# Index gather and gate weights of an expert layer in 16 bits, on VectorE alone

## The chip, the cores and the metric

The kernel runs on one core of a Trainium2 chip. Its metric is the time of one execution on the device in microseconds (us), the median of several runs. The engines are TensorE (PE; its weight loads are a row of their own, PEld), VectorE (DVE), ScalarE (ACT), GpSimd (POOL) and SyncE (SP), which here issues the loads. Each works through its own list of instructions in a fixed order; semaphores hold an instruction until its inputs are there and its output buffer is free.

## The reference, cut to what matters

The reference is two transformer blocks on 256 tokens of width 1024 in float32. The change lies in the last part of the second block, a feed-forward layer of product-key experts:

```python
q = (xb @ w_query).reshape(t, 8, 2, 64)              # 8 heads, 2 key halves
s = einsum('thpd,hpkd->thpk', q, sub_keys)           # 128 keys for each half
top_s, top_i = top_k(s, 16)
cand_s = top_s[:, :, 0, :, None] + top_s[:, :, 1, None, :]        # 16 x 16
cand_i = top_i[:, :, 0, :, None] * 128 + top_i[:, :, 1, None, :]
best_s, best_pos = top_k(cand_s, 16)
idx = take_along_axis(cand_i, best_pos, -1)          # 16 of 16384 experts
gate = softmax(best_s)
act = gelu(einsum('td,thkd->thk', xb, expert_down[idx]))
y = einsum('thk,thkd->td', gate * act, expert_up[idx])
```

## The kernel before, in words

The kernel doesn't fetch single experts. It multiplies all tokens with all 16384 rows of both expert tables and puts the gates in between as a matrix W, which is zero for every expert that a token did not choose. An expert's number is 128 i + j, with i from the first key half and j from the second. W lies with j on the 128 partitions, then i, then the token: 128 x 128 x 256, in two halves of 64 i (`W0`, `W1`).

**Weight stream.** All weights come in granules of 128 x 1024 float32 (`granule`, lines 199 to 216). SP loads one into `raw`; ACT rounds it to the format of the products (`wh`, line 214); a subtraction gives the rest (`wl`, line 215). A product is then the sum of three matmuls: wh with the high part of the other operand, wh with its low part, wl with the high part. `wl` runs on DVE, except where `B.share` is 2: then every second granule's goes to POOL. `raw` has 4 buffers, `wh` and `wl` 3 each.

**Down** (`down`, line 1204) takes two granules a step, 24 matmuls of 256 tokens for each (lines 239 to 241), and ACT writes the gelu of the sum into W. **Up** (`up`, line 1235) takes one granule for each i: ACT and DVE split W's row into `wsh` and `wsl` (lines 225 and 226), and 12 matmuls of 512 columns add to four accumulators that stay open over all 128 granules (lines 1248 to 1250).

**Selection** (`select`) runs beside the first half of down. For each of two blocks of 128 tokens it makes the scores (line 1120), sorts out the best 16 of each key half with `top16` (DVE, one input each), adds the 16 x 16 candidates on POOL (`cand`, line 1132) and sorts again. The index gather follows (lines 1140 to 1155): the position in the candidates gives two numbers of 0 to 15 (`pf`); each is compared with a `ramp` of 0 to 15, the result multiplied by the indices (`idf`) and summed over the 16 (`m`, 1024 elements of float32 at a time, four times a block). The end of a block transposes numbers and gates to (head, choice) on partitions (`finish`), and the gate times 4096 is split into two float16 parts.

**Gates** (`gates`, line 1212) go over 8 tokens at a time, 32 groups for each half of W. DVE compares i with a ramp (`eq`, 8 x 64) and j with a ramp (`a`, 8 x 128), both float16; ACT multiplies eq by the gate's high part, one instruction a token; POOL by its low part; PE adds, for each token, `a` (as weights) times `bh` (64 columns) for both parts (line 1227); DVE multiplies the PSUM result into W (line 1229), walking W by token, then i, so that neighbours are 1024 bytes apart.

The order of work comes from generators that are driven side by side with weights: `down(0)` with `select` (1.0 to 2.1), `down(64)` with `gates(0)` (1.0 to 1.25), `up(0)` with `gates(64)` (1.0 to 1.25), then `up(64)` alone. A scheduler with a cost model of its own then fixes the list of each engine.

Of the kernel before, what the change touches and what calls it, by code (L numbers as in the profile page):

```python
# [17 lines left out]
OP = mybir.AluOpType  # L18
# [13 lines left out]
# ---------------------------------------------------------------- host layout  # L32


def _blocks_b(w):
    """[K, N] -> granules [*, 128, 1024]: for each 128 columns all of K, on partitions."""
    k, n = w.shape
    g = w.reshape(k // P, P, n // P, P).transpose(2, 1, 0, 3)
    per = D // k
    g = g.reshape(n // P // per, per, P, k).transpose(0, 2, 1, 3)  # L40
    return g.reshape(-1, P, D)


def _blocks_a(w, width):
    """[K, N] -> granules [*, 128, 1024]: for each `width` columns, D / width chunks of K at a time."""
# [33 lines left out]
def pack(inputs):  # L79
# [38 lines left out]
    # by query (row, column): head, key row, key column  # L118
# [16 lines left out]
# ---------------------------------------------------------------- helpers  # L135


def bc(ap, n):
    """A view with an inner dimension of stride 0."""
    return bass.AP(tensor=ap.tensor, offset=ap.offset, ap=[list(s) for s in ap.ap] + [[0, n]])  # L140


def bc_at(ap, pos, n):
    """A view with a dimension of stride 0 put before dimension `pos`."""
# [4 lines left out]
def drive(*gens):  # L149
    """Interleaves generators in proportion to the weights they come with."""  # L150
# [10 lines left out]
class Block:  # L161
# [15 lines left out]
    # ------------------------------------------------------------ constants  # L177
# [20 lines left out]
    # ------------------------------------------------------------ weight stream  # L198
    def granule(self, src, kept=None):
        """Loads [128, 1024] of weights; returns the two exact parts for float32r products."""  # L200
# [32 lines left out]
    def mm_cols(self, out, w, x, nk, first=True, last=True, off=0):  # L233
        """out[n, t] += W[k, n] X[k, t]; w: two [128, 1024] parts, columns off ... of them."""
# [8 lines left out]
    def mm_rows(self, outs, w, x, k0, nk, width, first, last, off=0, tiles=(0, 1)):  # L243
        """outs[i][t, n] += X[k, t] W[k, n] over nk chunks of K from k0 on."""
# [11 lines left out]
    # ------------------------------------------------------------ norms  # L256
    def rsqrt(self, v, pool, tag):
        """v^-0.5 of a few columns, by Newton steps from the exponent's half."""
# [18 lines left out]
    def gain(self, pool, name, tag, bufs=1):  # L277
        """A gain in every partition, times the root of the row length."""
# [11 lines left out]
    def total(self, pool, ss, tag):  # L290
        """sum of squares + D eps of both row blocks, from the sums over halves."""
# [4 lines left out]
    def scaled_cols(self, pool, src, r, g, x, width=512):  # L296
        """(src * r) * g, rows to columns, in two parts; r: a column of each row block."""
# [8 lines left out]
    def warm(self, n):  # L306
        """Keeps the tensor engine's clock up while it waits for a norm."""
# [7 lines left out]
    def turn(self, y, x, k0, n, i):  # L315
        """n blocks of 128 columns of y to the columns x, from block k0 on."""
# [7 lines left out]
# ---------------------------------------------------------------- first block  # L324


def first_block(B, rp):
    tc, nc, A = B.tc, B.nc, B.A
    with ExitStack() as es:
# [11 lines left out]
        # the gain in every partition, times the root of the row length  # L341
# [113 lines left out]
        def conv():  # L455
# [3 lines left out]
            # layer norm over the channels  # L459
# [81 lines left out]
        # relative position bias of every query and key; -1e30 outside the window  # L541
# [5 lines left out]
        # twice the merged branches  # L547
# [24 lines left out]
    # ---------------- feed-forward  # L572
    with ExitStack() as es:
# [40 lines left out]
        # the final norm of this block and the first of the next one:  # L614
        # x3 = x2 r2 gf with r2 = (v / D)^-0.5, v = sum x2^2 + D eps, and
        # h3 = x3 r3 g3 with r2 r3 = (u / D)^-0.5, u = sum (x2 gf)^2 + eps v
# [36 lines left out]
def rows_out(B, rp, name, X, res, scale, g, X2, pool, tags):  # L653
    """res + scale * (X^T W), as rows; its normed columns go to X2."""
# [32 lines left out]
# ---------------------------------------------------------------- second block  # L687


def rope_tables(B, cp, pool):  # L690
    """sin and cos of position * frequency, [128 t, 2, 8] each."""
# [11 lines left out]
    # ang - 2 pi n, with n the nearest integer and 2 pi in three parts  # L703
# [603 lines left out]
```

## Time and profile before

| | |
|---|---|
| time, median of 3 runs | 1481.1 us (1480.63 to 1483.35) |
| span of the profiled execution | 1484.5 us |
| mean granted TensorE clock | 0.991 |
| PE, PEld busy | 97%, 88% |
| DVE, ACT, POOL busy | 76%, 59%, 19% |
| selection beside `down(0)` | about 690 to 885 us |
| `gates(0)` beside `down(64)` | to about 1108 us |
| `gates(64)` beside `up(0)` | to about 1272 us |
| `up(64)`, end | to 1484.5 us |

The profile is one execution; the span is from its first to its last instruction, and no time beside the span was taken of that execution. Groups of instructions read: line, engine, operation, output<-inputs, shapes, count | busy us, mean ns of one | idle time of the engine just before them, and who ended it. The timeline reads: start, duration, engine, line, operation, count, and in brackets the idle time before it.

### The profile page before, as it was taken

The page shows a single profiled execution, that of the slowest core. Times are in us where ns is not written, and L with a number is a line of the kernel's source. Part 1 is how long each engine was busy: PE and PEld are TensorE (multiplying, and loading weights), DVE is VectorE, ACT ScalarE, POOL GpSimd, SP SyncE. Part 2 cuts the span into 40 slices and gives each one's busy share as a digit, 9 for nine tenths or more (in the row PEclk, how much of TensorE's full clock was granted, in tenths as well). Part 3 has the DMA queues.
Part 4 walks back from the last instruction along what each step waited for, and adds up shares of the span by engine and source line. Part 5 has one row for each costly group of instructions (what it writes and reads, how often), then busy time and mean ns, then how long its engine had stood idle before and what let it go on. Part 6 is the DMA issues. An engine that isn't in the chain of part 4 may idle for free.

```text
span 1484.5 us, 27008 instructions
## 1 busy us (share of the span) xinstructions
PE 1440.6 (97%) x10351; PEld 1302.6 (88%) x10351; DVE 1134.0 (76%) x1812; ACT 881.8 (59%) x1697; POOL 286.5 (19%) x253
## 2 busy tenths in 40 slices
PE   8899999999999999999989989999999999999998
PEld 7788989999898888989989989999997777888887
DVE  6987867768796667764877876999959999765665
ACT  6476566566554666444444446877757777555453
POOL 4543000000203000002434542222103433000000
PEclk9999999999999999999999999999999999999999
DMA  7534556556466333565544445455565545666664
GB/s 257 172 109 143 180 177 189 183 186 225 123 191 203 120 110 111 178 205 162 166 150 156 156 150 171 157 168 167 165 213 157 157 157 157 199 193 191 198 192 135
DMA packets 70117, 251.49 MB, mean 169 GB/s; under 512 B 8026, under 2 KB 8418, under 8 KB 69731
## 3 DMA queue, kind: packets, MB, share of 16 engines
q1 hardware_dynamic: 69698, 249.17, 52.9%
q8 instruction: 81, 1.33, 0.4%
q10 hardware_dynamic: 288, 0.59, 0.2%
q14 instruction: 50, 0.40, 0.1%
HBM read 247.63 MB, written 2.11 MB: 168 GB/s over the span
## 4 chain that ended last, share of the span: by engine, by line
PE 84%; DVE 12%; issue 2%; ACT 1%; DMA 0%; POOL 0%; SPq 0%; POOLq 0%; ACTq 0%; DVEq 0%
PE mm L239 15%; PE mm L241 15%; PE mm L240 15%; PE mm L1250 7%; PE mm L1248 7%; PE mm L1249 7%; DVE wl L215 3%; PE mm L253 2%; PE mm L254 2%; PE mm L252 2%; PE at L1227 2%; DVE y L441 2%; PE at L585 1%; PE at L586 1%; PE at L587 1%
## 5 line engine op out<-in xcount | busy, mean ns | idle before, releaser
L214 ACT ACTIVATE wh<-raw 128x1024 fp32r<-128x1024 f32 (+1 forms) x457 | 479.8, 1052 | 360.2 <-PE mm L240 273.3
L215 DVE TENSOR_TENSOR wl<-raw,wh 128x1024 fp32r<-128x1024 f32 x422 | 531.3, 1261 | 204.2 <-ACT wh L214 198.5
L241 PE MATMUL mm<-xh,wl 128*128 128x256 f32 x1952 | 559.3, 287 | 16.5 <-DVE wl L215 16.5
L239 PE MATMUL mm<-xh,wh 128*128 128x256 f32 x1952 | 562.2, 288 | 0.9 <-ACT xh L225 0.9
L240 PE MATMUL mm<-xl,wh 128*128 128x256 f32 x1952 | 558.9, 286 | 0.0
L241 PEld LDWEIGHTS mm<-xh,wl 128*128 128x128 f32 x1952 | 378.7, 194 | 20.9 <-DVE wl L215 18.9
L239 PEld LDWEIGHTS mm<-xh,wh 128*128 128x128 f32 x1952 | 379.0, 194 | 7.3 <-issue 2.9
L240 PEld LDWEIGHTS mm<-xl,wh 128*128 128x128 f32 x1952 | 379.0, 194 | 4.3 <-issue 3.3
L1250 PE MATMUL mm<-wh,wsl 128*128 128x512 f32 x512 | 200.8, 392 | 6.3 <-DVE wsl L226 6.3
L1248 PE MATMUL mm<-wh,wsh 128*128 128x512 f32 x512 | 201.8, 394 | 0.0
L1249 PE MATMUL mm<-wl,wsh 128*128 128x512 f32 x512 | 199.8, 390 | 0.1
L1221 POOL TENSOR_TENSOR bh<-eq,parts 128x512 f16<-128x512 f16 x64 | 100.4, 1578 | 274.3 <-PE at L1227 172.8
L1220 ACT ACTIVATE bh<-eq,high 128x64 f16<-128x64 f16 x512 | 128.7, 334 | 16.0 <-DVE eq L1217 15.3
L225 ACT ACTIVATE wsh<-W 128x256 fp32r<-128x256 f32 x128 | 53.2, 417 | 127.9 <-PE mm L1249 125.7
L1250 PEld LDWEIGHTS mm<-wh,wsl 128*128 128x128 f32 x512 | 96.1, 188 | 30.6 <-DVE wsl L226 10.4
L1249 PEld LDWEIGHTS mm<-wl,wsh 128*128 128x128 f32 x512 | 96.2, 188 | 20.6 <-DVE wl L215 1.1
L1248 PEld LDWEIGHTS mm<-wh,wsh 128*128 128x128 f32 x512 | 96.2, 188 | 18.6
L215 POOL TENSOR_TENSOR wl<-raw,wh 128x1024 fp32r<-128x1024 f32 (+1 forms) x35 | 86.8, 2481 | 121.3 <-ACT wh L214 120.7
L1229 DVE SCALAR_TENSOR_TENSOR W<-at,W 128x512 f32<-128x512 f32 x64 | 84.5, 1341 | 10.2 <-PE at L1227 10.2
L226 DVE TENSOR_TENSOR wsl<-W,wsh 128x256 fp32r<-128x256 f32 x128 | 53.5, 418 | 42.1 <-ACT wsh L225 42.1
L1223 DVE TENSOR_TENSOR a<-ramp,numbers 128x1024 f16<-128x1024 f16 x64 | 79.9, 1250 | 0.0
L446 POOL TENSOR_TENSOR y<-y,tap 128x256 f32<-128x256 f32 x60 | 58.5, 975 | 51.4 <-ACT tap L445 47.3
(343 smaller groups left out, 1740.1 us busy)
## 6 DMA issues: line engine op xcount, KB each, us to landing
raw<-in_ws_dram SPq DMA_DIRECT2D x199, 512.0 KB, 3.6
raw<-in_pd_dram SPq DMA_DIRECT2D x128, 512.0 KB, 3.6
raw<-in_pu_dram SPq DMA_DIRECT2D x128, 512.0 KB, 3.6
bias<-in_rpb_dram SPq DMA_DIRECT2D x2, 1024.0 KB, 7.7
x<-in_x_dram SPq DMA_DIRECT2D x4, 256.0 KB, 4.0
r_m<-in_rows_dram SPq DMA_DIRECT2D x2, 512.0 KB, 3.6
mb<-negm_d SPq DMA_DIRECT2D x4, 256.0 KB, 5.4
x<-xn SPq DMA_DIRECT2D x2, 512.0 KB, 5.4
```

The source lines that it names most:

```text
L214: nc.scalar.activation(wh[:, c], raw[:, c], AF.Copy)
L215: eng.tensor_sub(wl[:, c], raw[:, c], wh[:, c].bitcast(F32))
L239: mm(out, wh[:, k], xh[:, k], start=(first and k == 0), stop=False)
L240: mm(out, wh[:, k], xl[:, k], start=False, stop=False)
L241: mm(out, wl[:, k], xh[:, k], start=False, stop=(last and k == nk - 1))
L1220: nc.scalar.activation(bh[:, 0, q], eq[:, q], AF.Copy, scale=B.high[:, t + q:t + q + 1])
L1221: nc.gpsimd.tensor_tensor(bh[:, 1], eq, bc(B.parts[:, 1, c], H), op=OP.mult)
L1223: nc.vector.tensor_tensor(a, bc_at(ramp, 1, 8), bc(jj[:, c], P), op=OP.is_equal)
L1229: nc.vector.scalar_tensor_tensor(w, g.rearrange("p (t i) -> p t i", t=8), 1.0 / 4096.0, w, op0=OP.mult, op1=OP.mult)
L1248: nc.tensor.matmul(a, wp[0][:, ts], u[0][:, ns], start=(i == 0), stop=False)
L1249: nc.tensor.matmul(a, wp[0][:, ts], u[1][:, ns], start=False, stop=False)
L1250: nc.tensor.matmul(a, wp[1][:, ts], u[0][:, ns], start=False, stop=(i == NE - 1))
```

## The change

What it does:

- The index gather works in float16 with the heads innermost. `ramp` is written out in full (16 x 128), `m` holds one key half of all 8 heads (2048 elements), and the sum over 16 is three halvings and a last addition in place of a reduction. `idx` and `pu` are read in steps when they are cast.
- In the gates two tokens lie innermost in `eq`, `a`, `bh`, and in the ramp (128 x 2); the numbers of 8 tokens are read as 4 pairs, each pair again and again along i or j. Both products with the gate's parts are DVE instructions of 512 elements; the ACT and POOL ones go, and `B.high` with them.
- The gate matmuls read `a` and `bh` in steps of two elements.
- W is multiplied with i outer and the 8 tokens inner; the PSUM result is read in steps of 64 elements.
- `B.share` stays 0: all residues `wl` of selection run on DVE.

```diff
-    ramp = pool.tile([P, K], F32, tag="ramp", name="ramp")
-    nc.gpsimd.iota(ramp, pattern=[[1, K]], base=0, channel_multiplier=0, allow_small_or_imprecise_dtypes=True)
+    ramp = pool.tile([P, K, 8 * K], F16, tag="ramp", name="ramp")
+    nc.gpsimd.iota(ramp, pattern=[[1, K], [0, 8 * K]], base=0, channel_multiplier=0,
+                   allow_small_or_imprecise_dtypes=True)
...
-        idf = pool.tile([P, 8, 2, K], F32, tag="idf", name="idf", bufs=2)
-        nc.vector.tensor_copy(idf, idx)
+        idf = pool.tile([P, 2, K, 8], F16, tag="idf", name="idf", bufs=2)
+        nc.vector.tensor_copy(idf, idx.rearrange("p h e k -> p e k h"))
...
-        pf = pool.tile([P, 2, 8, K], F32, tag="pf", name="pf", bufs=1)
-        nc.vector.tensor_copy(pf, pu)
+        pf = pool.tile([P, 2, K, 8], F16, tag="pf", name="pf", bufs=1)
+        nc.vector.tensor_copy(pf, pu.rearrange("p e h k -> p e k h"))
+        yield
         for pp in range(2):
-            for hq in range(0, 8, 4):
-                m = pool.tile([P, 4 * K, K], F32, tag="m", name="m", bufs=4)
-                m4 = m.rearrange("p (h k) a -> p h k a", h=4)
-                nc.vector.tensor_tensor(m, bc(pf[:, pp, hq:hq + 4].rearrange("p h k -> p (h k)"), K),
-                                        bc_at(ramp, 1, 4 * K), op=OP.is_equal)
-                nc.vector.tensor_tensor(m4, m4, bc_at(idf[:, hq:hq + 4, pp], 2, K), op=OP.mult)
-                nc.vector.tensor_reduce(res[:, pp, hq * K:(hq + 4) * K], m, axis=AX.X, op=OP.add)
-                yield
+            m = pool.tile([P, K, 8 * K], F16, tag="m", name="m", bufs=2)
+            nc.vector.tensor_tensor(m, ramp, bc_at(pf[:, pp].rearrange("p k h -> p (k h)"), 1, K), op=OP.is_equal)
+            m4 = m.rearrange("p a (k h) -> p a k h", h=8)
+            nc.vector.tensor_tensor(m4, m4, bc_at(idf[:, pp], 2, K), op=OP.mult)
+            yield
+            for n in (8, 4, 2):
+                nc.vector.tensor_tensor(m[:, 0:n], m[:, 0:n], m[:, n:2 * n], op=OP.add)
+            nc.vector.tensor_tensor(res[:, pp].rearrange("p (h k) -> p k h", h=8), m4[:, 0], m4[:, 1], op=OP.add)
+            yield
...
-    nc.vector.tensor_copy(B.high, B.parts[:, 0])
...
-        ramp = pool.tile([P, P], F16, name="ramp128")
+        ramp = pool.tile([P, P, 2], F16, name="ramp128")
...
-            ii, jj = B.numbers[:, 0], B.numbers[:, 1]
+            def pairs(v, n):
+                v = v.rearrange("p (a b) -> p a b", b=2)
+                return bc_at(v, 2, n)
+
             for t in range(0, T, 8):
                 c = slice(t, t + 8)
-                eq = B.pool2.tile([P, 8, H], F16, tag="eq", name="eq", bufs=2)
-                nc.vector.tensor_tensor(eq, bc_at(ramp[:, i0:i0 + H], 1, 8), bc(ii[:, c], H), op=OP.is_equal)
-                bh = B.pool2.tile([P, 2, 8, H], F16, tag="bh", name="bh", bufs=2)
-                for q in range(8):
-                    nc.scalar.activation(bh[:, 0, q], eq[:, q], AF.Copy, scale=B.high[:, t + q:t + q + 1])
-                nc.gpsimd.tensor_tensor(bh[:, 1], eq, bc(B.parts[:, 1, c], H), op=OP.mult)
-                a = B.pool2.tile([P, 8, P], F16, tag="a01", name="a01", bufs=2)
-                nc.vector.tensor_tensor(a, bc_at(ramp, 1, 8), bc(jj[:, c], P), op=OP.is_equal)
+                ii, jj = B.numbers[:, 0, c], B.numbers[:, 1, c]
+                eq = B.pool2.tile([P, 4, H, 2], F16, tag="eq", name="eq", bufs=2)
+                nc.vector.tensor_tensor(eq, bc_at(ramp[:, i0:i0 + H], 1, 4), pairs(ii, H), op=OP.is_equal)
+                bh = B.pool2.tile([P, 2, 4, H, 2], F16, tag="bh", name="bh", bufs=2)
+                for k in range(2):
+                    nc.vector.tensor_tensor(bh[:, k], eq, pairs(B.parts[:, k, c], H), op=OP.mult)
+                a = B.pool2.tile([P, 4, P, 2], F16, tag="a01", name="a01", bufs=2)
+                nc.vector.tensor_tensor(a, bc_at(ramp, 1, 4), pairs(jj, P), op=OP.is_equal)
                 g = B.bank("at")
                 for q in range(8):
                     for k in range(2):
-                        nc.tensor.matmul(g[:, q * H:(q + 1) * H], a[:, q], bh[:, k, q], start=(k == 0), stop=(k == 1))
-                w = W[i0 // H][:, :, c].rearrange("p i t -> p t i")
-                nc.vector.scalar_tensor_tensor(w, g.rearrange("p (t i) -> p t i", t=8), 1.0 / 4096.0, w, op0=OP.mult,
+                        nc.tensor.matmul(g[:, q * H:(q + 1) * H], a[:, q // 2, :, q % 2], bh[:, k, q // 2, :, q % 2],
+                                         start=(k == 0), stop=(k == 1))
+                w = W[i0 // H][:, :, c]
+                nc.vector.scalar_tensor_tensor(w, g.rearrange("p (t i) -> p i t", t=8), 1.0 / 4096.0, w, op0=OP.mult,
                                                op1=OP.mult)
...
-            B.share = 2
             drive((1.0, down(0)), (2.1, sel))
-            B.share = 0
```

The lists of the engines change at three places. First POOL, from the last norm of the second block into selection (`pw` is that norm's power, `cand` the candidates); the list of before, then that of now:

```order
L274 TENSOR_TENSOR pw<-v,mhalf 128x1
L1105 IOTA ramp 128x16
L274 TENSOR_TENSOR pw<-v,mhalf 128x1
L1200 IOTA ramp_7436 128x128
L215 TENSOR_TENSOR wl<-raw,wh 128x1024 x3
L1132 TENSOR_TENSOR cand<-top 128x256 x2
```

```order
L274 TENSOR_TENSOR pw<-v,mhalf 128x1
L1106 IOTA ramp 128x2048
L274 TENSOR_TENSOR pw<-v,mhalf 128x1
L1204 IOTA ramp_7435 128x256
L1134 TENSOR_TENSOR cand<-top 128x256 x16
```

The larger ramp stands between the two powers, as the small one did; of POOL's work in the experts only the candidates are left.

Second DVE at the first block's index gather, before and now:

```order
L1151 TENSOR_TENSOR m<-pf,ramp 128x1024 x2
L1153 TENSOR_TENSOR m<-m,idf 128x1024
L215 TENSOR_TENSOR wl<-raw,wh 128x1024
L1154 TENSOR_REDUCE res<-m 128x64
L1153 TENSOR_TENSOR m<-m,idf 128x1024
L1151 TENSOR_TENSOR m<-pf,ramp 128x1024
L1154 TENSOR_REDUCE res<-m 128x64
L215 TENSOR_TENSOR wl<-raw,wh 128x1024
```

```order
L1153 TENSOR_TENSOR m<-ramp,pf 128x2048 x2
L215 TENSOR_TENSOR wl<-raw,wh 128x1024
L1155 TENSOR_TENSOR m<-m,idf 128x2048
L215 TENSOR_TENSOR wl<-raw,wh 128x1024
L1158 TENSOR_TENSOR m<-m 128x1024
L1155 TENSOR_TENSOR m<-m,idf 128x2048
L215 TENSOR_TENSOR wl<-raw,wh 128x1024
L1158 TENSOR_TENSOR m<-m 128x512
L1158 TENSOR_TENSOR m<-m 128x1024
```

Before, three or four instructions of the gather stand between two residues, and POOL makes every second one; now one or two stand between them, or some of the short additions, and every residue is in this list.

Third DVE beside the first half of up (`wsl` is the low part of a row of W, `W` the product with the gates), before and now:

```order
L215 TENSOR_TENSOR wl<-raw,wh 128x1024
L226 TENSOR_TENSOR wsl<-W_7438,wsh 128x256
L1217 TENSOR_TENSOR eq<-ramp_7436,numbers 128x512
L215 TENSOR_TENSOR wl<-raw,wh 128x1024
L226 TENSOR_TENSOR wsl<-W_7438,wsh 128x256
L1229 SCALAR_TENSOR_TENSOR W_10083<-at,W_10083 128x8x64 x2
L1223 TENSOR_TENSOR a_14940<-ramp_7436,numbers 128x1024
L215 TENSOR_TENSOR wl<-raw,wh 128x1024
```

```order
L226 TENSOR_TENSOR wsl<-W_7437,wsh 128x256
L1239 SCALAR_TENSOR_TENSOR W_10077<-at,W_10077 128x64x8
L215 TENSOR_TENSOR wl<-raw,wh 128x1024
L1230 TENSOR_TENSOR bh<-eq,parts 128x512 x2
L1232 TENSOR_TENSOR a_13216<-ramp_7435,numbers 128x1024
L226 TENSOR_TENSOR wsl<-W_7437,wsh 128x256
L1227 TENSOR_TENSOR eq<-ramp_7435,numbers 128x512
L215 TENSOR_TENSOR wl<-raw,wh 128x1024
```

A group of gates has five DVE instructions now, three before, between the same residues.

More of the change, by code (lines that the diff above doesn't have):

```diff
@@ L1195, in experts @@
         xt = B.xt
-        B.high = pool.tile([P, T], F32, name="high")
         B.numbers = pool.tile([P, 2, T], F16, name="numbers")
         B.parts = pool.tile([P, 2, T], F16, name="parts")
-        ramp = pool.tile([P, P], F16, name="ramp128")
-        nc.gpsimd.iota(ramp, pattern=[[1, P]], base=0, channel_multiplier=0, allow_small_or_imprecise_dtypes=True)
+        ramp = pool.tile([P, P, 2], F16, name="ramp128")
+        nc.gpsimd.iota(ramp, pattern=[[1, P], [0, 2]], base=0, channel_multiplier=0,
+                       allow_small_or_imprecise_dtypes=True)
         H = NE // 2
```

## Prediction

> **What bounds the kernel now.** I read the page first, then the busy time of each engine by stretches, then the groups and waits inside the stretches that the change touches. The page puts TensorE ahead of all:
>
> ```profile
> PE 1440.6 (97%) x10351; PEld 1302.6 (88%) x10351; DVE 1134.0 (76%) x1812; ACT 881.8 (59%) x1697; POOL 286.5 (19%) x253
> ```
>
> So a gain can come only from places where TensorE waits. The change touches four stretches of the second block's experts: 690 to 890 us (selection beside the first half of down), 890 to 1108 (second half of down beside the first gates), 1108 to 1272 (first half of up beside the second gates), and from there the second half of up. The stretches (us, then PE, PEld, DVE, ACT, POOL busy with counts, clock, DMA share, GB/s):
>
> ```profile
> 690.00:738.00 48.00, 48.00 (x392) 46.98 (x391) 38.46 (x186) 22.63 (x27) 22.79 (x16) 1.00 0.54 167
> 738.00:772.00 34.00, 28.79 (x225) 28.18 (x224) 32.08 (x39) 15.65 (x18) 11.94 (x5) 0.96 0.44 150
> 772.00:834.00 62.00, 62.00 (x507) 60.95 (x506) 44.06 (x199) 27.25 (x34) 28.70 (x18) 1.00 0.52 162
> 834.00:864.00 30.00, 25.38 (x189) 24.97 (x188) 29.93 (x29) 13.31 (x15) 12.64 (x4) 0.90 0.40 131
> 864.00:890.00 26.00, 23.30 (x178) 22.91 (x178) 16.48 (x16) 12.56 (x26) 13.07 (x6) 0.92 0.47 170
> 890.00:1108.00 218.00, 218.00 (x2173) 216.16 (x2172) 176.77 (x168) 151.78 (x364) 40.27 (x34) 1.00 0.55 171
> 1108.00:1272.00 164.00, 157.61 (x1110) 124.22 (x1109) 163.46 (x189) 124.50 (x340) 59.83 (x30) 1.00 0.52 162
> ```
>
> PE's busy time hides part of its waits (each matmul's modelled end covers its neighbour's start), so I count matmuls. In the chain in order of time the 32 gate matmuls of two groups take 0.95 us, and in the last stretch 512-wide matmuls run without a wait:
>
> ```profile
> 908.26 0.95 PE at L1227 x32
> ```
>
> ```profile
> 1280.00:1440.00 160.00, 160.00 (x707) 1.00 0.63 194
> ```
>
> That is 0.95/32 = 0.0297 us for a gate matmul and 160/707 = 0.2263 for one of up. From 890 to 1108 all 32 groups of the first gates run, 512 matmuls or 15.2 us; the other 1661 share 202.8 us, 0.1221 each. At that pace 738 to 772 loses 34 - 225 x 0.1221 = 6.5 us, 834 to 864 loses 6.9, 864 to 890 loses 4.3: **17.7 us in selection**, and none in 690 to 738 or 890 to 1108. For 1108 to 1272, by groups (count | busy, mean ns), PE and then DVE:
>
> ```profile
> L1248 PE MATMUL mm<-wh,wsh 128*128 128x512 f32 x200 | 80.4, 402 | 0.0
> L1250 PE MATMUL mm<-wh,wsl 128*128 128x512 f32 x199 | 79.1, 397 | 6.3 <-DVE wsl L226 6.3
> L1249 PE MATMUL mm<-wl,wsh 128*128 128x512 f32 x199 | 78.0, 392 | 0.1
> L1227 PE MATMUL at<-bh,a 128*128 128x64 f16 x512 | 19.3, 193 | 0.0
> ```
>
> ```profile
> L215 DVE TENSOR_TENSOR wl<-raw,wh 128x1024 fp32r<-128x1024 f32 x50 | 60.4, 1209 | 0.5 <-ACT wh L214 0.5
> L1229 DVE SCALAR_TENSOR_TENSOR W<-at,W 128x512 f32<-128x512 f32 x32 | 42.0, 1332 | 0.0
> L1223 DVE TENSOR_TENSOR a<-ramp,numbers 128x1024 f16<-128x1024 f16 x30 | 36.3, 1208 | 0.0
> L226 DVE TENSOR_TENSOR wsl<-W,wsh 128x256 fp32r<-128x256 f32 x49 | 20.0, 409 | 0.5 <-ACT wsh L225 0.5
> L1217 DVE TENSOR_TENSOR eq<-ramp,numbers 128x512 f16<-128x512 f16 x28 | 18.9, 676 | 0.0
> ```
>
> 598 x 0.2263 + 512 x 0.0297 = 150.5 of 164: **13.5 us lost**, and DVE is busy for 163.46 of the 164, so DVE is the bound there. Its five groups sum to 177.6 over 189 instructions: each begins 0.075 us before the one ahead ends, and I take 75 ns off every DVE duration. The waits name the same cause in both places (total, times, longest):
>
> ```profile
> PE mm L241 <- DVE wl L215: 12.5, 6, 2.7
> ```
>
> ```profile
> PE mm L1250 <- DVE wsl L226: 6.3, 10, 1.0
> ```
>
> Why DVE is late in selection the timeline shows, DVE first, POOL below:
>
> ```profile
> 743.17 4.45 DVE L1151 TENSOR_TENSOR m<-pf,ramp 128x1024 f32<-128x1024 f32 x2
> 748.68 3.40 DVE L215 TENSOR_TENSOR wl<-raw,wh 128x1024 fp32r<-128x1024 f32 x1
> 756.53 3.05 DVE L215 TENSOR_TENSOR wl<-raw,wh 128x1024 fp32r<-128x1024 f32 x1
> ```
>
> ```profile
> 742.48 2.92 POOL L215 TENSOR_TENSOR wl<-raw,wh 128x1024 fp32r<-128x1024 f32 x1 [3.35 <-ACT wh L214]
> 748.29 2.71 POOL L215 TENSOR_TENSOR wl<-raw,wh 128x1024 fp32r<-128x1024 f32 x1 [2.88 <-ACT wh L214]
> 756.10 2.41 POOL L215 TENSOR_TENSOR wl<-raw,wh 128x1024 fp32r<-128x1024 f32 x1 [5.09 <-ACT wh L214]
> ```
>
> A two-input DVE instruction that meets POOL's residue ends when POOL's does: a wl of 1.2 us takes 3.40.
>
> **The change part by part.** All changed rows run on DVE, so I price a 16-bit instruction there. No row shows a two-input one whose operands all step together. Upper bound: eq as it is, 676 ns (0.601 net). Lower bound, the nearest row of 512 16-bit results at half that:
>
> ```profile
> L1178 DVE CAST numbers<-picks 128x512 f16<-128x512 f32 x1 | 0.4, 421 | 0.0
> L1176 DVE CAST parts<-picks 128x256 f16<-128x256 f32 x1 | 0.3, 286 | 0.0
> ```
>
> Its slope is (421 - 286)/256 = 0.53 ns, so net 0.346 for 512, 0.616 for 1024, 1.155 for 2048, 0.211 for 256. I take the lower: eq and a now read a number over and over, and exactly that reading goes. [...]
>
> *Gates.* W is now read and written in runs of 8 tokens, and PSUM in steps of 64 instead. A product from PSUM without any steps:
>
> ```profile
> L509 DVE SCALAR_TENSOR_TENSOR s<-at,bias 128x512 f32<-128x512 f32 x8 | 5.5, 682 | 1.7 <-PE at L506 1.7
> ```
>
> Two stepping operands cost 1332 - 682 = 650 ns; one should cost half, so 1.007 us, net 0.932, between 0.607 and 1.257 (nothing excludes more). The 512 ACT instructions and 64 POOL ones vanish; their work comes to DVE as two of 512 a group. From 1108 to 1272 DVE then needs 50 wl x 1.134 + 49 wsl x 0.334 + 32 W x 0.932 + 30 a x 0.616 + 28 eq x 0.346 + 60 bh x 0.346 = 56.7 + 16.4 + 29.8 + 18.5 + 9.7 + 20.8 = 151.9 us, and PE 150.5. The 164 falls to about 154 with 2 left for uneven bursts: **-10**, from -1 (W at 1.257) to -13.5 (PE's floor). From 890 to 1108 PE never waits: **0**.
>
> *Selection.* In 738 to 772 DVE held:
>
> ```profile
> L215 DVE TENSOR_TENSOR wl<-raw,wh 128x1024 fp32r<-128x1024 f32 x5 | 12.1, 2417 | 0.0
> L1151 DVE TENSOR_TENSOR m<-pf,ramp 128x1024 f32<-128x1024 f32 x4 | 6.9, 1738 | 0.0
> L1153 DVE TENSOR_TENSOR m<-m,idf 128x1024 f32<-128x1024 f32 x4 | 4.8, 1209 | 0.0
> L1154 DVE TENSOR_REDUCE res<-m 128x64 f32<-128x1024 f32 x4 | 4.8, 1205 | 0.0
> ```
>
> The 16.5 of m become, for each key half, 2 x 1.155 + 0.616 + 0.346 + two of about 0.21, in all 7.4; idf and pf are read in steps now, some 0.5 more. POOL's wl come over: 225/24 = 9.4 granules x 1.134 = 10.7 instead of 12.1. So 32.08 - 16.5 - 12.1 + 7.4 + 0.5 + 10.7 = 22 us for work that PE does in 27.5: the stall goes, as do those of 834 to 890, which POOL's holds made too. The price stands where DVE sorts: 690 to 738 gets 8 wl more, 38.46 + 9.1 = 47.5 of 48 us, and 772 to 834 gets 507/48 = 10.6, 44.06 + 12.0 = 56.1 of 62. A full engine in fixed order is late now and then, with three buffers of wl as the only reserve, and cand's short POOL instructions still hold a wl sometimes. I leave 4 us: **-13.7**, from 0 to -17.7.
>
> *Ramp.* The iota grows from 16 to 2048 elements and stands on POOL ahead of the last norm's pw, for which PE waits:
>
> ```profile
> 656.91 0.14 POOL L1105 IOTA ramp<- 128x16 f32 x1 [3.44 <-DMA x<-xn]
> 658.51 0.55 POOL L274 TENSOR_TENSOR pw<-v,mhalf 128x1 f32<-128x1 f32 x1 [1.46 <-DVE v L293]
> 664.34 0.24 POOL L1200 IOTA ramp<- 128x128 f16 x1 [5.27 <-PE at L319]
> ```
>
> 0.1 us for 112 elements more makes 0.14 + 1.8 us for 2048; begun at 656.91 it ends near 658.9, and pw starts 0.4 later: **+0.4**, 0 to 2. The second ramp grows to 256 elements behind that pw and is first read by the gates, 200 us on: 0.
>
> *Strided operands of the gate matmuls.* They step 4 bytes. The loads' row, and the plain 4-byte one:
>
> ```profile
> L1227 PEld LDWEIGHTS <-a 128*128 128x128 f16 x1024 | 32.6, 98 | 7.7 <-issue 5.8 <-DVE a L1223 0.8
> L240 PEld LDWEIGHTS mm<-xl,wh 128*128 128x128 f32 x1952 | 379.0, 194 | 4.3 <-issue 3.3
> ```
>
> I take 98 to stay: the type is the same, and the load lies under the matmul ahead. If it became 194, see below.
>
> Sum: -10 - 13.7 + 0.4 = -23.3. The profiled span is 1484.5, 3.4 above the median 1481.1 of the runs; I set the same difference against the median: **1458 us**.
>
> **The rivals.**
> A, the sum above: 1450 to 1466; chance 0.55.
> B, PSUM steps cost DVE what W's steps did: W stays at 1.257, DVE needs 162, that stage gains 1 instead of 10: 1467. For it, no row reads PSUM in steps; against it, only one operand of three steps. [...] Chance 0.14.
> C, selection becomes DVE's: at 47.5 of 48 the sorting stretches lose 10 us more: 1468. Chance 0.13.
> D, slower: 16-bit instructions stay at 0.601 for 512, as both 16-bit rows of before run. From 1108 to 1272 DVE needs 56.7 + 16.4 + 29.8 + 34.0 + 16.8 + 36.1 = 190, 26 over the 164; from 890 to 1108 0.88 more a group, 176.77 + 28 = 205 of 218, say 5; selection gains 10: 1481 + 21 = 1502. It decides from where 512 elements cost over 0.42 net (wl, wsl and W 103; 88 of eq and bh and 30 of a at 1.9 times that: 103 + 145x = 164). Chance 0.10.
> E, slower: the strided load takes 194 ns and a gate matmul the 0.1221 of those that follow such loads: 1.48 a group, 47 us from 890 to 1108, and PE 198 instead of 164 after it, so 47 + 34 - 14: 1548. Chance 0.04.
> That all gains are eaten up is left 0.04. The change does what it says: every instruction of it is in the order.
>
> **How the numbers follow.** 1458 is A's. The range runs from 1448 (17.7 + 13.5 off and a little for the spread of the runs) to 1472, past B and C, which holds 0.82. About 0.2%, 3 us, can be told from no change. Faster A + B + C = 0.82, same 0.04, slower D + E = 0.14.
>
> **What would show it.** Right: bh rows on DVE near 420 ns, m of 2048 near 1230, W near 1010; no wl over 1.9 us; under 6 us lost in selection and about 3 from the second gates on; the gate loads at 98. Wrong: eq still at 676 (D), loads over 98 (E), W over 1300 (B), PE waiting for wl while DVE sorts (C).

## The result

The changed kernel takes **1455.86 us** (median of 4 runs, 1454.76 to 1456.41), the kernel before 1482.15 in the same comparison (4 runs, 1480.63 to 1483.35): a ratio of 0.982, 95% interval 0.9807 to 0.9832, or 26.3 us less. The forecast was 1458.0 with a range of 1448 to 1472. The profiled execution of the changed kernel took 1454.76 us with a span of 1453.0; the one of before has a span of 1484.5, above most of its runs, so the two traces differ by 31.5 us where the medians differ by 26.3.

First the engines over the whole span:

```profile
PE 1429.1 (98%) x10351; PEld 1297.6 (89%) x10351; DVE 1092.5 (75%) x1971; ACT 761.2 (52%) x1185; POOL 110.2 (8%) x157
```

TensorE executes as many matmuls as before and is busy for 11.5 us less, because a wait counts in part as busy (the six of before's selection are 13.5 us by the starts of its matmuls and 12.5 as idle time) and because some matmuls of before ran at a granted clock of 0.50 (shown under x5). ACT lost 120 us of work and POOL 176; neither had been near full (59% and 19%).

Next the groups by line and shape, in the order: count, busy us, mean ns of one, idle time ahead of them. These rows answer to the prices of the prediction:

```profile
L1230 DVE TENSOR_TENSOR bh<-eq,parts 128x512 f16<-128x512 f16 x128 | 48.8, 418 | 0.0
L1232 DVE TENSOR_TENSOR a<-ramp,numbers 128x1024 f16<-128x1024 f16 x64 | 43.8, 684 | 0.0
L1239 DVE SCALAR_TENSOR_TENSOR W<-at,W 128x512 f32<-128x512 f32 x64 | 42.7, 686 | 22.5 <-PE at L1236 22.3
L1236 PEld LDWEIGHTS <-a 128*128 128x128 f16 x1024 | 33.5, 98 | 7.6 <-issue 6.5
L1227 DVE TENSOR_TENSOR eq<-ramp,numbers 128x512 f16<-128x512 f16 x64 | 26.0, 417 | 0.0
```

The 16-bit instructions stand where they were priced (421 and 691 with their overlap), and the strided weight loads stay at 98 ns. W's product is at 686 ns instead of 1007: it costs what the product from PSUM without any steps cost in the trace of before, 682.

The stretches, in the columns of the prediction (us, then PE, PEld, DVE, ACT, POOL busy, clock, DMA share, GB/s); they end a little elsewhere, since the work moved:

```profile
690.00:738.00 48.00, 48.00 (x391) 46.99 (x391) 45.28 (x187) 23.11 (x28) 5.80 (x8) 1.00 0.49 154
738.00:772.00 34.00, 33.48 (x278) 33.14 (x277) 27.80 (x52) 17.71 (x20) 0.00 (x0) 1.00 0.61 188
772.00:834.00 62.00, 62.00 (x510) 61.08 (x509) 58.93 (x219) 28.69 (x36) 6.79 (x8) 1.00 0.55 163
834.00:870.00 36.00, 36.00 (x303) 36.00 (x302) 27.07 (x42) 17.86 (x20) 0.00 (x0) 1.00 0.64 190
1082.00:1240.00 158.00, 158.00 (x1131) 128.87 (x1130) 144.47 (x251) 70.38 (x104) 0.00 (x0) 1.00 0.58 177
```

From 738 to 772 TensorE issued 278 matmuls where it had issued 225, and 278 x 0.1221 = 33.9 of 34 us: the index gather hardly stalls it now (the longest distance between two matmuls is 0.80 us). In the sorting stretches VectorE is nearly full (45.28 of 48, 58.93 of 62) and is late nowhere. In the last row, up beside the second gates, VectorE has 13.5 us to spare and TensorE none.

Three distances in the timeline divide the experts into the stages of the change: from the first to the 33rd gelu of down (selection beside it), from the 33rd to the 64th (the first gates beside it), and from the first matmul of up to that of its 65th granule 32 steps later (the second gates beside it). With the kernels of the experiments, in us; medians are over 4 runs or more:

| kernel | selection | first gates | second gates | median |
|---|---|---|---|---|
| before | 213.7 | 195.5 | 202.95 | 1482 to 1484 |
| changed | 194.5 | 196.1 | 192.7 | 1455.9 |
| x1 GpSimd's residues back | 202.1 | 196.1 | 192.7 | 1463.0 |
| x2 W by token | 194.55 | 196.1 | 199.2 | 1462.4 |
| x3 no pairs | 194.5 | 199.75 | 227.1 | 1492.5 |
| x4 float32 gather | 199.7 | 196.1 | 192.7 | 1460.3 |
| x5 before, no residues on GpSimd | 198.2 | 195.5 | 203.1 | 1469.4 |
| x6 before, W along rows | 209.9 | 195.5 | 205.9 | 1484.4 |
| x7 no low part of the gate | 194.5 | 188.4 | 185.1 | 1441.1 |
| x8 16 tokens a step | 194.5 | 195.3 | 191.8 | 1453.6 |
| x11 x6 without GpSimd's product | 207.8 | 195.5 | 192.5 | 1466.7 |
| x12 before without GpSimd's product | 207.8 | 195.5 | 202.8 | 1478.7 |

So 19.2 us of the trace's 31.5 lie in selection and 10.3 beside the second gates, and the first gates take 0.6 back. The other 2.7 lie ahead of the first gelu and are no gain of the change: a norm's power (`pw`) far ahead of every edit starts at 390.52 us before and at 387.85 now, and at 387.94 in x12, whose code is that of before up to there. Selection's size needs care too: before, x6, x11 and x12 select in the same way and show 207.8 to 213.7 (the reason is under x11 and x12).

### The profile page after: what moved, and what is told of

The parts are those of the page before. It is cut to its first block, busy times and chain, and to the rows that moved or that the text cites. A ratio compares the mean times of both kernels' runs of the same rounds, so it can differ in the third digit from the quotient of the medians.

```text
span 1453.0 us, 26393 instructions
## 1 busy us (share of the span) xinstructions
PE 1429.1 (98%) x10351; PEld 1297.6 (89%) x10351; DVE 1092.5 (75%) x1971; ACT 761.2 (52%) x1185; POOL 110.2 (8%) x157
## 4 chain that ended last, share of the span: by engine, by line
PE 89%; DVE 7%; issue 1%; ACT 1%; DMA 1%; POOL 1%; SPq 0%; POOLq 0%; ACTq 0%
PE mm L239 16%; PE mm L240 16%; PE mm L241 16%; PE mm L1258 8%; PE mm L1260 8%; PE mm L1259 8%; PE at L1236 2%; PE mm L253 2%; DVE wl L215 2%; PE mm L254 2%; PE mm L252 2%; DVE y L441 2%; PE at L585 1%; PE at L586 1%; PE at L587 1%
## 5 line engine op out<-in xcount | busy, mean ns | idle before, releaser
L215 DVE TENSOR_TENSOR wl<-raw,wh 128x1024 fp32r<-128x1024 f32 x454 | 558.1, 1232 | 202.9 <-ACT wh L214 197.0
L1260 PE MATMUL mm<-wh,wsl 128*128 128x512 f32 x512 | 199.7, 390 | 0.0
L1259 PEld LDWEIGHTS mm<-wl,wsh 128*128 128x128 f32 x512 | 96.3, 188 | 19.2
L253 PE MATMUL mm<-wl,xh 128*128 128x512 f32 (+1 forms) x160 | 61.1, 382 | 0.6 <-DVE wl L215 0.6
L254 PE MATMUL mm<-wh,xl 128*128 128x512 f32 (+1 forms) x160 | 61.1, 382 | 0.2 <-DVE xl L226 0.2
L252 PE MATMUL mm<-wh,xh 128*128 128x512 f32 (+1 forms) x160 | 61.1, 382 | 0.0
L1239 DVE SCALAR_TENSOR_TENSOR W<-at,W 128x512 f32<-128x512 f32 x64 | 42.7, 686 | 22.5 <-PE at L1236 22.3
L1230 DVE TENSOR_TENSOR bh<-eq,parts 128x512 f16<-128x512 f16 x128 | 48.8, 418 | 0.0
```

The costliest lines, as they stand in the source:

```text
L215: eng.tensor_sub(wl[:, c], raw[:, c], wh[:, c].bitcast(F32))
L252: mm(outs[i], xh[:, k0 + k, ts], wh[:, k], start=st, stop=False)
L253: mm(outs[i], xh[:, k0 + k, ts], wl[:, k], start=False, stop=False)
L254: mm(outs[i], xl[:, k0 + k, ts], wh[:, k], start=False, stop=en)
L1259: nc.tensor.matmul(a, wp[0][:, ts], u[1][:, ns], start=False, stop=False)
L1260: nc.tensor.matmul(a, wp[1][:, ts], u[0][:, ns], start=False, stop=(i == NE - 1))
```

## The experiments

The theory has two parts. Selection gains because GpSimd's residues no longer hold VectorE's two-input instructions, with the lighter gather helping. Up gains because VectorE's load falls below TensorE's, which takes the 16-bit pairs and the order of W together. The rivals give each gain to one edit alone.

### Selection: x1, x4, x5

x1 is the changed kernel with GpSimd's residues in selection:

```diff
+            B.share = 2
             drive((1.0, down(0)), (2.1, sel))
+            B.share = 0
```

> The changed kernel with GpSimd's residues put back during selection alone. Theory (selection's gain is that GpSimd's residues no longer hold VectorE's two-input instructions): slower by about 5 us (3 to 10), wl instructions over 1.9 us come back beside the residues, and the idle ahead of the down matmuls that ends at wl returns. Rival (selection's gain is the lighter float16 index gather): slower by 1 us at most, because two in five residues are then off VectorE and the gather stays light.

Measured: 1462.98 us (1462.02 to 1463.87), 7.1 more than the changed kernel. All of it is in selection (202.1 against 194.5). Two groups of 690 to 880 us, then one row of VectorE's timeline and one of GpSimd's:

```profile
L215 POOL TENSOR_TENSOR wl<-raw,wh 128x1024 fp32r<-128x1024 f32 x30 | 76.0, 2533 | 93.6 <-ACT wh L214 92.8 <-POOL cand L1134 0.7
L1153 DVE TENSOR_TENSOR m<-ramp,pf 128x2048 f16<-128x2048 f16 x4 | 8.9, 2272 | 0.1
```

```profile
746.21 3.40 DVE L215 TENSOR_TENSOR wl<-raw,wh 128x1024 fp32r<-128x1024 f32 x1
```

```profile
745.61 2.92 POOL L215 TENSOR_TENSOR wl<-raw,wh 128x1024 fp32r<-128x1024 f32 x1 [2.67 <-ACT wh L214]
```

The product m of 2048 takes 2272 ns on the mean instead of 1221, and a wl takes 3.40 again. VectorE has the lighter gather and fewer residues to make, and TensorE still waits longer (6.2 us for wl in this stretch against 0.5): the rival falls. The two timeline rows show the hold: VectorE's wl begins 0.60 us behind GpSimd's, which ends at 748.53, and ends 1.08 us after it, about what a wl takes alone (1.2).

x4 is the changed kernel with the index gather of before (float32, `ramp` of 16, four quarters `m`, a reduction), and no residues on GpSimd:

```diff
-            m = pool.tile([P, K, 8 * K], F16, tag="m", name="m", bufs=2)
...
+            for hq in range(0, 8, 4):
+                m = pool.tile([P, 4 * K, K], F32, tag="m", name="m", bufs=4)
...
```

> The changed kernel with the index gather in float32 as before, and still no residues on GpSimd. Theory (VectorE fits selection without GpSimd's hold, the gather is only part of its load): slower by 5 us (3 to 8). Rival (the gather made the whole gain of selection): slower by 14 to 19 us, all of it before the 33rd gelu.

Measured: 1460.34 us (1459.62 to 1461.03), 4.5 more than the changed kernel, selection 199.7. The gather is worth about 5 us once GpSimd is out of the way.

x5 takes the one line `B.share = 2` out of the kernel before:

```diff
-            B.share = 2
             drive((1.0, down(0)), (2.1, sel))
```

> The kernel before with GpSimd's residues taken away and nothing else. Theory (GpSimd's residues hold VectorE's): faster by 10 to 13 us, no wl over 1.9 us in selection, the idle ahead of the down matmuls falls from 16.5 us to some 6. Rival (GpSimd's residues relieve VectorE, which is short in selection): no change or slower.

Measured: 1469.43 us (1468.18 to 1470.26) against 1483.54, a ratio of 0.991 (0.9891 to 0.9928), or 14.1 us less: somewhat more than the theory's 10 to 13. TensorE's third product in 690 to 880 us, of before, x5 and the changed kernel, with the wait for wl at the end of the row:

```profile
L241 PE MATMUL mm<-xh,wl 128*128 128x256 f32 x455 | 131.5, 289 | 9.8 <-DVE wl L215 9.8
```

```profile
L241 PE MATMUL mm<-xh,wl 128*128 128x256 f32 x486 | 137.8, 284 | 3.2 <-DVE wl L215 3.2
```

```profile
L241 PE MATMUL mm<-xh,wl 128*128 128x256 f32 x496 | 140.7, 284 | 0.5 <-DVE wl L215 0.5
```

The wait falls from 9.8 to 3.2 without GpSimd, and to 0.5 with the light gather as well. So one deleted line brings 14.1 us and the gather 4.5 more, 18.6 in all. The order matters for who gets the credit: with GpSimd still there (before against x1) the two traces differ by 11.6 in selection.

The waits are not the whole loss. In the selection stage of before, six distances between matmuls are long (1.76 to 2.98 us, 13.5 in all over the usual distance). Behind four of the six the granted clock falls to 0.50, here behind the last one, which begins at 880.74 (us, PE busy with count, clock, DMA share, GB/s):

```profile
882.00:884.00 2.00, 0.28 (x2) 1.00 0.00 0
884.00:886.00 2.00, 2.00 (x15) 0.76 0.56 145
886.00:888.00 2.00, 2.00 (x12) 0.50 1.02 412
888.00:890.00 2.00, 2.00 (x17) 0.89 0.62 229
890.00:892.00 2.00, 2.00 (x19) 1.00 0.00 0
```

At a clock of 1.00 a matmul of down begins 0.120 us after the one ahead, at 0.50 it is 0.213. Some 16 matmuls a time cost 1.5 us, the four times 6. The changed kernel has one distance of 0.80 us and no such time. So of selection's 19.2 us some 13 were waits and 6 the clock behind them.

### Up: x2, x3, x7

x2 walks W by token again, as before:

```diff
-                w = W[i0 // H][:, :, c]
-                nc.vector.scalar_tensor_tensor(w, g.rearrange("p (t i) -> p i t", t=8), 1.0 / 4096.0, w, op0=OP.mult,
+                w = W[i0 // H][:, :, c].rearrange("p i t -> p t i")
+                nc.vector.scalar_tensor_tensor(w, g.rearrange("p (t i) -> p t i", t=8), 1.0 / 4096.0, w, op0=OP.mult,
```

> The changed kernel with W's product walked by token again, everything else as changed. Theory (up's gain is VectorE's load falling below TensorE's): the product is back at about 1257 ns, VectorE needs some 156 us of work in the 32 up groups where TensorE needs 152, slower by 4 to 8 us. Rival (the order of W alone made the whole gain of up, the 16-bit pairs none): slower by 10 us or more.

Measured: 1462.36 us (1461.73 to 1463.02), 6.5 more, all beside the second gates (199.2 against 192.7), where VectorE became the bound again. That stretch (PE, PEld, DVE, ...) and W's row:

```profile
1085.00:1245.00 160.00, 157.31 (x1109) 123.99 (x1108) 158.16 (x249) 68.53 (x100) 0.00 (x0) 1.00 0.54 167
```

```profile
L1239 DVE SCALAR_TENSOR_TENSOR W<-at,W 128x512 f32<-128x512 f32 x64 | 84.7, 1345 | 14.5 <-PE at L1236 14.5
```

x3 undoes the pairs: one number is repeated along the inner dimension, both products stay on VectorE, and `a` and `bh` lie in a row for TensorE.

```diff
-                eq = B.pool2.tile([P, 4, H, 2], F16, tag="eq", name="eq", bufs=2)
-                nc.vector.tensor_tensor(eq, bc_at(ramp[:, i0:i0 + H], 1, 4), pairs(ii, H), op=OP.is_equal)
+                eq = B.pool2.tile([P, 8, H], F16, tag="eq", name="eq", bufs=2)
+                nc.vector.tensor_tensor(eq, bc_at(ramp[:, i0:i0 + H], 1, 8), bc(ii, H), op=OP.is_equal)
...
-                nc.vector.tensor_tensor(a, bc_at(ramp, 1, 4), pairs(jj, P), op=OP.is_equal)
+                nc.vector.tensor_tensor(a, bc_at(ramp, 1, 8), bc(jj, P), op=OP.is_equal)
```

> The changed kernel with tokens not paired: each number repeated along the inner dimension with a stride of zero, both products still on VectorE. Theory (two different 16-bit numbers innermost halve the price): eq and the products back at about 676 ns, a at about 1208, VectorE at some 176 us of work against TensorE's 152 in up and over it beside the first gates too, slower by 30 us (20 to 42). Rival (16 bits alone bring half the price, whatever is innermost): no change.

Measured: 1492.48 us (1491.36 to 1493.36), 36.6 more than the changed kernel and slower than before (ratio 1.0067, 1.0048 to 1.0085). Beside the second gates it is 227.1 against 192.7; the first gates lose 3.7 too. VectorE's 16-bit groups from 1095 to 1270 us, then that stretch (PE, PEld, DVE, ...):

```profile
L1229 DVE TENSOR_TENSOR bh<-eq,parts 128x512 f16<-128x512 f16 x57 | 36.9, 685 | 0.0
L1231 DVE TENSOR_TENSOR a<-ramp,numbers 128x1024 f16<-128x1024 f16 x29 | 35.4, 1219 | 0.0
L1226 DVE TENSOR_TENSOR eq<-ramp,numbers 128x512 f16<-128x512 f16 x27 | 18.5, 685 | 0.0
```

```profile
1095.00:1270.00 175.00, 161.11 (x1019) 121.52 (x1017) 168.22 (x233) 66.85 (x96) 0.00 (x0) 0.95 0.46 138
```

The type is the same as in the changed kernel, but bh takes 685 ns instead of 418 and a 1219 instead of 684; from 512 to 1024 elements the time grows by 534 ns instead of 267, twice as much. Two different numbers innermost are what halves it, and without that the move of the products to VectorE would have made the kernel slower.

x7 asks what bounds the changed kernel. It leaves out the 8 matmuls of a group that add the low part of the gate:

```diff
-                    for k in range(2):
-                        nc.tensor.matmul(g[:, q * H:(q + 1) * H], a[:, q // 2, :, q % 2], bh[:, k, q // 2, :, q % 2],
-                                         start=(k == 0), stop=(k == 1))
+                    nc.tensor.matmul(g[:, q * H:(q + 1) * H], a[:, q // 2, :, q % 2], bh[:, 0, q // 2, :, q % 2],
+                                     start=True, stop=True)
```

> The changed kernel without the 8 matmuls of each group that add the gate's low part (VectorE still forms both products; the low part of the gate is left out of the output). Theory (TensorE is what the expert part now goes by): faster by 15 us (13 to 16), 512 matmuls of about 29.7 ns. Rival (VectorE still sets the pace of up): faster by 7.6 us at most, from the down half alone.

Measured: 1441.1 us (1439.82 to 1442.32), 14.8 less. Half of it (7.7) lies beside the first gates, half (7.6) beside the second, as 512 matmuls of 29.7 ns should. TensorE is what the experts go by now; VectorE follows at this pace too, at 139.81 busy us of 145:

```profile
1080.00:1225.00 145.00, 145.00 (x849) 116.48 (x848) 139.81 (x248) 68.22 (x100) 0.00 (x0) 1.00 0.56 185
```

### The order of W alone: x6, x11, x12

x6 is the kernel before with W along its rows, the reverse of x2's edit and nothing else.

> The kernel before with W written along its rows and nothing else. Theory (the product's steps through W in SBUF are its price, reading PSUM in steps costs nothing): the product falls from 1257 to about 690 ns and up is 8 to 11 us faster, since VectorE falls below TensorE there. Rival (up's gain needs the 16-bit pairs too): 0 to 3 us faster.

Measured: 1484.41 us (1482.06 to 1487.48) against 1483.54, a ratio of 1.0011 (1.0 to 1.0022): no gain. The theory was wrong by 8 us or more. The rival's 0 to 3 us is nearer, but its reason isn't the right one either: x11 below reaches the changed kernel's time beside the second gates without pairs (it leaves a product out). The theory's price of W was right, as x6's groups from 1110 to 1270 us show, VectorE first and GpSimd's product behind it:

```profile
L215 DVE TENSOR_TENSOR wl<-raw,wh 128x1024 fp32r<-128x1024 f32 x49 | 67.8, 1383 | 0.5 <-ACT wh L214 0.5
...
L226 DVE TENSOR_TENSOR wsl<-W,wsh 128x256 fp32r<-128x256 f32 x48 | 28.2, 587 | 0.2 <-ACT wsh L225 0.2
L1217 DVE TENSOR_TENSOR eq<-ramp,numbers 128x512 f16<-128x512 f16 x28 | 24.1, 859 | 0.0
L1229 DVE SCALAR_TENSOR_TENSOR W<-at,W 128x512 f32<-128x512 f32 x30 | 19.8, 676 | 0.0
```

```profile
L1221 POOL TENSOR_TENSOR bh<-eq,parts 128x512 f16<-128x512 f16 x28 | 43.3, 1552 | 111.9 <-DVE eq L1217 59.5 <-DVE wsl L226 39.2 <-PE at L1227 13.2
```

W's product fell by 656 ns, over its 32 instructions 21 us. But wl rose from the 1209 of before to 1383, wsl from 409 to 587 and eq from 676 to 859: 49 x 0.174 + 48 x 0.178 + 28 x 0.183 = 22 us. The timelines show how, before ahead of x6, VectorE ahead of GpSimd in each:

```profile
1182.47 1.21 DVE L215 TENSOR_TENSOR wl<-raw,wh 128x1024 fp32r<-128x1024 f32 x1
1183.60 0.41 DVE L226 TENSOR_TENSOR wsl<-W,wsh 128x256 fp32r<-128x256 f32 x1
1183.94 1.32 DVE L1229 SCALAR_TENSOR_TENSOR W<-at,W 128x512 f32<-128x512 f32 x1
```

```profile
1182.23 2.68 POOL L1221 TENSOR_TENSOR bh<-eq,parts 128x512 f16<-128x512 f16 x1 [3.24 <-PE at L1227]
```

```profile
1183.22 2.06 DVE L215 TENSOR_TENSOR wl<-raw,wh 128x1024 fp32r<-128x1024 f32 x1
1185.20 1.26 DVE L226 TENSOR_TENSOR wsl<-W,wsh 128x256 fp32r<-128x256 f32 x1
```

```profile
1182.70 3.48 POOL L1221 TENSOR_TENSOR bh<-eq,parts 128x512 f16<-128x512 f16 x2 [4.63 <-DVE wsl L226]
```

Before, GpSimd's product begins just ahead of wl, takes 2.68 us and ends beside W's product, which reads PSUM and is not stretched (1.32 us; x12, which has no product on GpSimd, shows 1.325 on the mean). In x6 two of GpSimd's products run on end beside wl and wsl, and those take 2.06 and 1.26. W's long product had been their cover. This was formed as a theory after x6 and put to two kernels, which both leave GpSimd's product out, one with W along its rows and one by token:

```diff
-                nc.gpsimd.tensor_tensor(bh[:, 1], eq, bc(B.parts[:, 1, c], H), op=OP.mult)
...
-                        nc.tensor.matmul(g[:, q * H:(q + 1) * H], a[:, q], bh[:, k, q], start=(k == 0), stop=(k == 1))
+                        nc.tensor.matmul(g[:, q * H:(q + 1) * H], a[:, q], bh[:, 0, q], start=(k == 0), stop=(k == 1))
```

> The kernel before with W written along its rows and GpSimd's product for the gate's low part taken away (the low part is left out of the output; the matmuls that added it take the high part a second time, so TensorE's work stays). Theory (with W along its rows GpSimd's product runs beside wl, wsl and eq and stretches them by 21 us in the up groups, as much as the W order saved): wl back at 1208 ns, wsl at 408 and eq at 676 there, and 10 to 14 us faster than the kernel before. Rival (something else holds up the kernel with W along its rows): within 3 us of the kernel before.

> The kernel before with GpSimd's product for the gate's low part taken away, W still written by token (the low part is left out in the same way). Theory (in the kernel before, GpSimd's product runs beside the W product, which reads PSUM and isn't stretched, so it costs VectorE nothing): within 2 us of the kernel before. Rival (GpSimd's product costs VectorE time whatever it runs beside): faster by 5 us or more.

Measured: x11 1466.67 us (1465.03 to 1467.21), x12 1478.66 (1477.09 to 1481.03), the kernel before 1482.41 in the same comparison. Beside the second gates x11 needs 192.5 us, 13.4 less than x6, and x12 202.8, as before (202.95). So there GpSimd's product costs nothing with W by token and the whole gain with W along its rows. x11's rows in up, from 1110 to 1260 us:

```profile
L215 DVE TENSOR_TENSOR wl<-raw,wh 128x1024 fp32r<-128x1024 f32 x49 | 59.6, 1217 | 2.5 <-ACT wh L214 2.5
...
L226 DVE TENSOR_TENSOR wsl<-W,wsh 128x256 fp32r<-128x256 f32 x49 | 20.5, 419 | 7.8 <-ACT wsh L225 7.6
```

Over the whole kernel the two came out 15.7 and 3.75 us below before, 1.7 more than the theory's ranges allow in each case. In the traces the surplus lies in the selection stage (207.8 against 213.7). Selection's own code is the same, but the first groups of gates reach into this stage, and in before GpSimd's products stand there between its residues. VectorE's wl ahead of the last long wait, then GpSimd:

```profile
880.29 3.38 DVE L215 TENSOR_TENSOR wl<-raw,wh 128x1024 fp32r<-128x1024 f32 x1
```

```profile
877.80 2.02 POOL L1221 TENSOR_TENSOR bh<-eq,parts 128x512 f16<-128x512 f16 x1
879.78 2.80 POOL L215 TENSOR_TENSOR wl<-raw,wh 128x1024 fp32r<-128x1024 f32 x1
```

x6 has this wait too (2.97 us), x11 and x12 don't. The rest is the clock: it falls to 0.50 four times in before's selection and twice in each of the other three, 3 us less. So a part of x12's gain seems to be its own edit at work: GpSimd's product costs nothing beside the second gates, but something where the first groups meet the end of selection. How much was not tested by itself. x12 as a whole decides for neither side (it stays under the rival's 5 us); for up the stage itself decides.

### W's price taken apart: x9, x10

x9 reads W by token and writes a contiguous scratch tile, so W stays without its gates; x10 reads a contiguous tile of ones and writes W by token, so the activations are left out.

```diff
-                w = W[i0 // H][:, :, c]
-                nc.vector.scalar_tensor_tensor(w, g.rearrange("p (t i) -> p i t", t=8), 1.0 / 4096.0, w, op0=OP.mult,
+                w = W[i0 // H][:, :, c].rearrange("p i t -> p t i")
+                o = B.pool2.tile([P, 8, H], F32, tag="scr", name="scr", bufs=2)
+                nc.vector.scalar_tensor_tensor(o, g.rearrange("p (t i) -> p t i", t=8), 1.0 / 4096.0, w, op0=OP.mult,
```

> The changed kernel with the product reading W by token (in steps of 1 KB through SBUF) and writing a contiguous scratch tile; W itself is left ungated. Theory (reading and writing in steps each cost half of the 570 ns between 1257 and 686): about 0.97 us each. Rival (only one side costs): 1.26 us if it is the read, 0.69 us if it is the write.

> The changed kernel with the product reading a contiguous tile of ones in place of W and writing W by token; the product with the activations is left out. Theory (reading and writing in steps each cost half): about 0.97 us each. Rival (only one side costs): 1.26 us if it is the write, 0.69 us if it is the read.

Measured, x9 and then x10 (one run each; the price is that of 64 instructions):

```profile
L1240 DVE SCALAR_TENSOR_TENSOR scr<-at,W 128x512 f32<-128x512 f32 x64 | 67.6, 1074 | 19.4 <-PE at L1236 19.4
```

```profile
L1240 DVE SCALAR_TENSOR_TENSOR W<-at,scr 128x512 f32<-128x512 f32 x64 | 67.3, 1087 | 20.7 <-PE at L1236 20.7
```

Over 686 ns, reading in steps of 1 KB costs 388 and writing in them 401; both together cost 659 (x2). It is neither side alone. It isn't an even half either: half of 659 is 330, and each by itself costs some 60 to 70 ns more. (The theory's 0.97 us is 0.1 us too low, in part because its 1257 has the overlap of 75 ns taken off and its 686 hasn't.)

### Fewer turns between gate and weight matmuls: x8

x8 makes the operands of two groups, then issues both groups' matmuls, then both W products, with three buffers of `a` and `bh` and one of `eq`:

```diff
-            for t in range(0, T, 8):
+            for t0 in range(0, T, 16):
+                bhs, as_ = [], []
+                for t in (t0, t0 + 8):
...
+                for r in range(2):
+                    a, bh = as_[r], bhs[r]
+                    g = B.bank("at")
...
-                yield
+                yield 2.0
```

> The changed kernel with 16 tokens in each step of the gates instead of 8, so that TensorE changes between gate and weight matmuls 32 times instead of 64. Theory (each change costs TensorE about 0.09 us and TensorE is the bound): faster by 3 us (1 to 6). Rival (longer bursts on VectorE hold up the residues): no change or slower.

Measured: 1453.63 us (1453.14 to 1454.43), 2.2 under the changed kernel's median; its runs lie below all of the changed kernel's (1454.76 to 1456.41), though in another comparison. The traces give 0.8 and 0.9 us in the two gate stages, 1.7 / 32 = 0.05 for each turn saved, where the theory had 0.09. It is the fastest of the kernels that compute everything (ratio to before 0.980, 0.9782 to 0.9818), but by less than the 3 us that the prediction takes as the least to be told from no change.

## Why the prediction was right

- *What bounds the kernel.* Right: TensorE waited in selection, and VectorE was the bound beside the second gates. x7 shows that TensorE is the bound in both gate stages now. The 17.7 us in selection were too few. Their pace of 0.1221 came from a stretch with turns to gate matmuls in it; without those it is 0.120, and the trace has 13.5 us of waits and 6 of half clock, which the prediction counted with the waits without naming it.
- *GpSimd's hold.* Right in its price of 3.40 us, but the reading that a two-input VectorE instruction "ends when POOL's does" is wrong: the wl shown for it ends at 752.08 and GpSimd's at 751.00, so it ends 1.08 us later, about a wl's own 1.2, as if it had waited for the whole of GpSimd's.
- *Prices in 16 bits.* Right: 418 ns for bh and 417 for eq (421 forecast), 684 for a (691), 1221 for m of 2048 (1230). Taking the lower of the two bounds was the author's choice, as no row of before had such an instruction. x3 shows the reason for it to be the right one: 685 and 1219 with a repeated number. From 512 to 1024 elements the time grows by 267 ns with pairs and by 534 without.
- *W's product.* Mis-sized: 1007 ns forecast, 686 measured. The step that failed is "one should cost half". It gave PSUM's steps half the price of W's, and they cost 4 ns (686 against 682); all of the price was in reading and writing W in SBUF (388 and 401 ns alone in x9 and x10, 659 together in x2).
- *Gates beside up, -10.* Right in number, -10.3, but not by the sum that gave it, so the agreement is luck. VectorE was expected at 151.9 us, just over TensorE, with 2 us added for uneven bursts. It came out with room to spare, and the gain ends at TensorE's floor, which lies higher than the 150.5 us from which the bound of -13.5 came: 1131 matmuls of 1082 to 1240 are 619 x 0.2263 + 512 x 0.0297 = 155.3 of 158 us, and the other 2.7 go with 32 turns to gate matmuls and back (behind the bursts at 1149.83 and 1155.79 the second matmul of up follows after 0.32 us, not 0.23). These had been counted as lost to VectorE. An error of 10 us in VectorE's price of W and one of 2.7 in TensorE's floor, with the 2 us for bursts, came to the same 154.
- *First gates, 0.* Nearly: 0.6 us longer in the trace.
- *Selection, -13.7.* Right in mechanism, short in size. x5 and x4 give 14.1 + 4.5 = 18.6, the trace 19.2 (15.4 if x6 stands for before), more than the 17.7 given as the most. The "4 us left" for a full engine in fixed order were not there: VectorE ran at 94% and 95% of the sorting stretches and TensorE waited 0.5 us for wl.
- *Ramp, +0.4.* Right: the iota takes 1.93 us and TensorE's gap ahead of the last normed columns grew from 2.08 to 2.37.
- *Strided gate loads, 0.* Right, 98 ns.
- *The rivals.* B fell with the 686 ns, C with the 0.5 us, E with the 98 ns. D fell with the 417 ns, but x3 is D built: it forecast 26 us more beside the second gates and 5 more beside the first, and x3 shows 24.2 and 4.3 over before. Its price was right, its condition wasn't met.

What the prediction didn't see is the interplay in up. It treated the order of W, the move of the products and the pairs as terms that add. The order of W alone brings nothing (x6) because GpSimd's product then loses its cover; the move without the pairs costs 10 us against before even with selection's gain (x3). Only because GpSimd's product went at the same time could W's order pay. Taking ScalarE's products away brought nothing by itself there: x11 keeps them and needs 192.5 us.

## What to carry to other kernels

Before giving GpSimd a share of elementwise work, look in the timeline at what VectorE does beside it: here a two-input instruction from SBUF was held by it (a wl of 1.2 us took up to 3.40), one fed from PSUM was not (1.32), and the shorter PSUM-fed instruction uncovered what it had hidden. Let a transposing walk fall on the PSUM side of a VectorE instruction and keep SBUF in runs (686 ns here, against 1345 with W by token in x2). If a 16-bit broadcast must be made, put two different numbers innermost (418 ns for 512 elements here, against 685 in x3); then price the engine's whole load against TensorE's count in that stage, since nothing below it is worth more.

## What was not expected of the hardware

- VectorE reads float32 from PSUM in steps of 64 elements at no cost that shows: 686 ns for 512 against 682 in a row.
- Walking W in SBUF in steps of 1 KB costs 388 ns per 512 elements read and 401 written, and 659 for both at once; runs of 8 elements cost nothing that shows (the same 686 against 682).
- GpSimd's product of 512 16-bit elements took 2.00 us on the mean in up before and 1.55 in x6. Before, the product was the longer one where the two met (2.68 us beside a wl of 1.21 that began 0.24 us after it); in x6 VectorE's wl was (2.06). What decides between the two these rows don't show.
- A turn to gate matmuls and back costs TensorE about 0.05 to 0.09 us, an estimate from x8's saving (1.7 us for 32 turns) and from the 2.7 us left over for 32 turns in up.
- A wait of TensorE cost more than its length in four cases of six. Behind four waits of 2.12 to 2.98 us the granted clock stood at 0.50 and the matmuls lost 1.5 us more; behind two others, of 2.17 and 1.76 us, it did not. What decides was not tested.
